# Streaming operands stored as two halves and read alternately, 16 columns from each

## The chip, the core and the metric

The kernel runs on one core of one Trainium2 chip. A core has a matrix engine (TensorE, called PE in the profile; its weight loads are listed apart, as PEld), three engines for elementwise work (VectorE = DVE, ScalarE = ACT, GpSimd = POOL), and queues that issue transfers (SP and POOL here). The on-chip memory that the engines read, SBUF, has 128 partitions; a tile [128, n] keeps n elements in each. Matrix results land in another memory, PSUM. The metric is the device time of one execution in microseconds: the median of three runs before the change is 1984.05 us (1983.36 to 1985.76).

A matrix instruction has two operands. One, 128 x 128 here, is loaded into the array and stays there (the *stationary* operand, the PEld rows). The other runs through the array column by column (the *streamed* or moving operand, 256 or 512 columns here). This case is about where the columns of the streamed operand lie in SBUF and in what order they are read.

## What is computed

One layer over 2048 tokens of width 1024, everything in float32:

```python
hl  = rms_norm(x) * A1 + sh1                      # A1, sh1 from the vector c and ada_w
b, cc, v = split(hl @ w_in, 3)                    # 1024 -> 3 x 1024
y   = (b * conv3(cc * v)) @ w_out
lat = x + g1 * y
h2  = rms_norm(lat) * A2 + sh2
aff = softmax(h2 @ router)                        # 16 experts
for e in range(16):                               # the 256 tokens with the highest aff[:, e]
    xs  = h2[idx[e]]
    hid = silu(xs @ w_gate[e]) * (xs @ w_up[e])
    out[idx[e]] += g2 * gate[e] * (hid @ w_down[e])
```

The kernel makes each large product in three parts. A float32 operand is split into a high part (written in the type float32r) and a low part (the rest), and high x high, low x high and high x low are summed in PSUM. So each operand exists twice, and each pair of tiles costs three matrix instructions.

## The kernel before

The work has four stages with large products, and the order of all instructions is written out by hand; each engine runs its own list in that order.

*Input projection* (`to_hl`, `in_mm`, `in_out`). Tokens are taken in four quarters of 512. `to_hl` transposes a normalised 128-channel slice of a quarter into PSUM (L383), and writes it as the tile `hl`: `t[:, 0]` is the high part, by ScalarE from PSUM (L386), `t[:, 1]` the low part, by VectorE or, for some tiles of the first quarter, by GpSimd (L389). `hl` is streamed, 512 columns at a time, against 128 x 128 pieces of `w_in` that are stationary (L436, L437, L439). This makes 2304 matrix instructions of 512 columns.

*Output projection and router* (`out_mm`, `router_mm`). Here the activations are stationary and the weight `w_out` is streamed, 512 columns at a time (L641, L642, L644; 768 instructions). Residual, second norm and router run behind it.

*Choice of tokens* (`search_few`, `search_all`, `slots`, `pick`). Thresholds are searched on VectorE and ScalarE; from 835 to 876 us of the span the matrix engine is busy for 10.7 of 41 us.

*Experts* (`gate_up`, `down`). For each of 16 experts the 256 chosen tokens are gathered and transposed into `xT` (`fetch`, L988 and L989). `gate_up` streams `xT`, 256 columns, against stationary pieces of `w_gate` and `w_up` (L1010, L1012, L1014; 6144 instructions). Its results go through L1020 to L1024 into `hT`, high and low. `down` holds `hT` stationary and streams `w_down`, 512 columns (L1032 to L1034; 1536 instructions).

Weights arrive as pieces of 128 x 1024 float32 in a list whose order is fixed: `load_piece` starts the transfer into `raw` (3 buffers), `split_high` copies it as the high part into `ws` (8 buffers, ScalarE, L198), `split_low` writes the low part (VectorE, now and then GpSimd, L208). A piece of `w_in`, `w_gate` or `w_up` is later stationary, a piece of `w_out` or `w_down` is streamed. In all of them the columns lie one behind the other, and every streamed operand is read as one run of 1024 or 2048 bytes per partition, for example

```python
t = hl_tile([P, 2, QT])
nc.tensor.matmul(ps[m], wh, t[:, 0], start=(k == 0), stop=False)
...
nc.tensor.matmul(o, w[:, 0, j, c0], xT[:, 0, k], start=(k == 0 and f % 2 == 0), stop=False,
...
nc.tensor.matmul(ps[s], h, w[:, 0, j], start=(k == 0), stop=False)
```

Of the kernel before, what the change touches and what calls it, by code (L numbers as in the profile page):

```python
# [16 lines left out]
P = 128  # L17
D = 1024
L = 2048
E = 16  # L20
CAP = 256
KD = D // P
NB = L // P
NQ = 4
QT = L // NQ
# [9 lines left out]

def dram(src, offset, ap):
    return bass.AP(tensor=src.tensor, offset=src.offset + offset, ap=ap)


@with_exitstack  # L40
def block_kernel(ctx: ExitStack, tc, x, c, ada_w, ada_b, norm_g, w_in, conv, w_out, router, wg, wu, wd, out):
    nc = tc.nc
    ctx.enter_context(tc.manual_schedule())
    consts = ctx.enter_context(tc.tile_pool(name="consts", bufs=1))
    wpool = ctx.enter_context(tc.tile_pool(name="weights", bufs=1))
# [3 lines left out]
    n_raw, n_split = 3, 8  # L49
# [39 lines left out]
    A1 = consts.tile([P, 8], F32, name="A1")  # L89
    sh1 = consts.tile([P, 8], F32, name="sh1")  # L90
# [77 lines left out]


    pieces, n_load, n_high, n_done = [], 0, 0, 0  # L170
    ws_of = {}
# [15 lines left out]
    def load_to(i):  # L187
        nonlocal n_load
        while n_load <= min(i, len(pieces) - 1, load_end[0] - 1):
            load_piece(n_load)  # L190
            n_load += 1

    def split_high(i):
        nonlocal n_high
        while n_high <= min(i, len(pieces) - 1):
            load_to(n_high)
            t = wpool.tile([P, 2] + pieces[n_high][3], F32R, name="ws", tag="ws", bufs=n_split)
            nc.scalar.activation(t[:, 0], raws[n_high], AF.Copy)  # L198
            ws_of[n_high] = t
            n_high += 1  # L200

    def split_low(i, eng=None, part=0, n=1):
        nonlocal n_done
        split_high(i)
        t, raw = ws_of[i], raws[i]
        w = pieces[i][3][-1] // n
        s = slice(part * w, (part + 1) * w)
        (eng or nc.vector).tensor_sub(t[:, 1, ..., s], raw[..., s], t[:, 0, ..., s].bitcast(F32))  # L208
        if part == n - 1:
            raws.pop(i)  # L210
            n_done += 1
            load_to(i + n_raw)

    def split_to(i, eng=None):
        while n_done <= min(i, len(pieces) - 1):
# [32 lines left out]
    w_o = [add_piece(w_out, k * P * D, [[D, P], [1, D]], [D]) for k in range(KD)]  # L248
    w_moe = {}

    def add_moe(m, e, h):
        for kk in range(KD // 2):
            for mm_ in (m if isinstance(m, tuple) else (m,)):
                w_moe[mm_, e, h, kk] = add_piece((wg, wu, wd)[mm_], (e * D + 2 * kk * P) * D + h * QT,
                                                 [[D, P], [P * D, 2], [1, QT]], [2, QT])

    for e in range(E + 1):
        for h in range(2):
# [89 lines left out]
    with tc.tile_pool(name="mix", bufs=1) as mix:  # L348
# [31 lines left out]
        def to_hl(q, k, between=lambda: None, eng=None):  # L380
            pt = tp.tile([P, QT], F32, name="pt", tag="tp")
            for b in range(4):
                nc.tensor.transpose(pt[:, b * P:(b + 1) * P], xq[q][b][:, k * P:(k + 1) * P], identf)  # L383
            full = m2("full")
            t = hl_tile([P, 2, QT])
            nc.scalar.activation(t[:, 0], pt, AF.Identity, scale=A1[:, k:k + 1], bias=sh1[:, k:k + 1])  # L386
            nc.scalar.activation(full, pt, AF.Identity, scale=A1[:, k:k + 1], bias=sh1[:, k:k + 1])
            between()
            (eng or nc.vector).tensor_sub(t[:, 1], full, t[:, 0].bitcast(F32))  # L389
            hl[q, k] = t  # L390

        ada_t, ada_a = {}, {}

# [36 lines left out]
            nc.vector.tensor_mul(A1[:, k:k + 1], A1[:, k:k + 1], g0_col[:, k:k + 1])  # L430

        def in_mm(ps, q, W, k):
            t = hl[q, k]
            for m in range(3):
                wh, wl = W(k, m)
                nc.tensor.matmul(ps[m], wh, t[:, 0], start=(k == 0), stop=False)  # L436
                nc.tensor.matmul(ps[m], wl, t[:, 0], start=False, stop=False)  # L437
            for m in range(3):
                nc.tensor.matmul(ps[m], W(k, m)[0], t[:, 1], start=False, stop=(k == KD - 1))  # L439

        def in_out(ps, q, ct):
            pb, pc, pv = ps
# [120 lines left out]
        before, ones_b, tri, slot_r, step, bias, need, zero1, cnts, aux, same, quick = constants(m2)  # L563
# [11 lines left out]
        for i, (ps_, ct, q) in enumerate(steps):  # L575
# [23 lines left out]
            ps = new_banks()  # L599
# [15 lines left out]
        def half(h):  # L615
            return slice(h * QT, (h + 1) * QT)
# [17 lines left out]
        def out_mm(tb, k, hs=(0, 1)):  # L634
            ps = ps_of.setdefault(tb, {})
            vh, vl = vs_of[tb]
            w = ws_of[w_o[k]]
            for h in hs:
                if k == 0:
                    ps[h] = mm.tile([P, QT], F32, name="pm", tag="mm")  # L640
                nc.tensor.matmul(ps[h], vh[:, k], w[:, 0, half(h)], start=(k == 0), stop=False)  # L641
                nc.tensor.matmul(ps[h], vh[:, k], w[:, 1, half(h)], start=False, stop=False)  # L642
            for h in hs:
                nc.tensor.matmul(ps[h], vl[:, k], w[:, 0, half(h)], start=False, stop=(k == KD - 1))  # L644

        def out_res(tb, h, soon=None):

# [343 lines left out]
    def gate_up(e, fh, between=lambda k: None):  # L991
        xT = xT_of[e]
        if fh == 0:
            hT_of[e] = {}
        ps = [[mm.tile([P, 2, CAP], F32, name="pm", tag="mm") for _ in range(2)] for _ in range(2)]
        for kk in range(KD // 2):
            for j in range(2):
                k = 2 * kk + j
                n = w_moe[0, e, fh, kk] + n_split - 2 + j
                if (e, fh) != (0, 1):  # L1000
                    split_high(n)
                between(k)
                while n_done <= min(n, len(pieces) - 1):
                    split_low(n_done, nc.gpsimd if n_done % 2 and (e, fh) < (1, 1) else None)
                for f in range(4):
                    c0 = slice(f * P, (f + 1) * P)
                    for m in range(2):
                        o = ps[m][f // 2][:, f % 2]
                        w = ws_of[w_moe[m, e, fh, kk]]
                        nc.tensor.matmul(o, w[:, 0, j, c0], xT[:, 0, k], start=(k == 0 and f % 2 == 0), stop=False,  # L1010
                                         skip_group_check=True)
                        nc.tensor.matmul(o, w[:, 0, j, c0], xT[:, 1, k], start=False, stop=False,  # L1012
                                         skip_group_check=True)
                        nc.tensor.matmul(o, w[:, 1, j, c0], xT[:, 0, k], start=False, stop=(k == KD - 1),  # L1014
                                         skip_group_check=True)
        hT = moe.tile([P, 2, 4, CAP], F32R, name="hT", tag="hT", bufs=4)
        hT_of[e][fh] = hT
        for f2 in range(2):
            sg = moe.tile([P, 2, CAP], F32, name="sg", tag="sg", bufs=2)
            nc.scalar.activation(sg, ps[0][f2], AF.Silu)  # L1020
            nc.vector.tensor_mul(sg, sg, ps[1][f2])
            t = slice(2 * f2, 2 * f2 + 2)
            nc.scalar.activation(hT[:, 0, t], sg, AF.Copy)
            nc.vector.tensor_sub(hT[:, 1, t], sg, hT[:, 0, t].bitcast(F32))  # L1024

    def down(e, dh, between=lambda kk: None):
        ps = [mm.tile([P, H], F32, name="pm", tag="mm") for _ in range(2)]

        def product(s, k):
            w, j, t = ws_of[w_moe[2, e, dh, k // 2]], k % 2, slice(s * P, (s + 1) * P)  # L1030
            h, l = (hT_of[e][k // 4][:, i, k % 4, t] for i in range(2))
            nc.tensor.matmul(ps[s], h, w[:, 0, j], start=(k == 0), stop=False)  # L1032
            nc.tensor.matmul(ps[s], h, w[:, 1, j], start=False, stop=False)  # L1033
            nc.tensor.matmul(ps[s], l, w[:, 0, j], start=False, stop=(k == KD - 1))  # L1034

        for kk in range(KD // 2):
            between(kk)
# [12 lines left out]
        c0 = slice(dh * H, (dh + 1) * H)  # L1050
# [75 lines left out]
```

## Time and profile before

| what | value |
|---|---|
| median of three runs | 1984.05 us |
| the profiled execution, whole | 1985.33 us |
| its span, first to last instruction | 1983.5 us |
| mean granted TensorE clock in the span | 0.982 |
| PE busy | 1901.4 us (96%) |
| PEld busy | 1669.5 us (84%) |
| DVE busy | 1130.6 us (57%) |
| ACT busy | 751.2 us (38%) |
| POOL busy | 306.9 us (15%) |
| moved by the transfers | 344.38 MB, 174 GB/s on average |

A row of a group of instructions reads: line of the kernel, engine, operation, tile written <- tiles read, shape, count | busy us, mean duration of one in ns | idle time of the engine just before them. Matrix instructions overlap in the array: the next starts while the last is still draining, so the duration of one is longer than the time from its start to the next one's start. It is that distance between starts that adds up to the length of a stage. The view of stretches gives for a window A:B its length, the busy time of each engine with the number of instructions that lie in it or are cut by its edges, the granted clock of the matrix engine (1.00 is full), the share of the transfer engines and GB/s. A row of the timeline gives the start in us from the span's start, the duration in us, and the instruction.

### The profile page before, as it was taken

The numbers are of one execution on the slowest core, as the hardware profiler recorded it, in microseconds if no ns is written. First come the engines' busy times: TensorE is split into PE (matmuls) and PEld (weight loads), VectorE is DVE, ScalarE is ACT, GpSimd is POOL, SyncE is SP. The second block draws the span as 40 slices with busy tenths as digits, with TensorE's granted clock in tenths as the row PEclk, the third lists the DMA queues.
The fourth block names the chain that finished last, engine by engine and source line by source line (L and its number), as shares of the span: only waits on it lengthen the run. The fifth ranks groups of instructions, "written<-read, shape, count | busy, mean of one in ns | idle before, by whom it ended". The sixth has DMA issues, their size and how long they took to land.

```text
span 1983.5 us, 29691 instructions
## 1 busy us (share of the span) xinstructions
PE 1901.4 (96%) x11930; PEld 1669.5 (84%) x11930; DVE 1130.6 (57%) x1656; ACT 751.2 (38%) x1050; POOL 306.9 (15%) x521
## 2 busy tenths in 40 slices
PE   4999999999999999659999999999999999999998
PEld 3787788887788888549999999999999999999996
DVE  7544424344334666776665656656665666566653
ACT  3411126211123333345444544444444444444542
POOL 3310011101011222333211011101110110111001
PEclk8999999999999999869999999999999999999999
DMA  9443241433216443235677676767677766777674
GB/s 283 127 133 127 81 144 53 139 127 123 67 64 213 166 149 132 85 127 165 199 222 211 214 233 200 220 217 235 202 214 233 227 201 214 229 209 218 212 212 116
DMA packets 216573, 344.38 MB, mean 174 GB/s; under 512 B 12092, under 2 KB 94068, under 8 KB 216436
## 3 DMA queue, kind: packets, MB, share of 16 engines
q1 hardware_dynamic: 200468, 284.82, 44.6%
q0 software_dynamic: 15968, 57.68, 11.2%
q8 instruction: 93, 1.52, 0.3%
q14 instruction: 44, 0.36, 0.1%
HBM read 300.51 MB, written 41.94 MB: 173 GB/s over the span
## 4 chain that ended last, share of the span: by engine, by line
PE 92%; DVE 3%; DMA 2%; SPq 1%; issue 1%; ACT 1%; POOL 0%; POOLq 0%; DVEq 0%; ACTq 0%
PE pm L1010 11%; PE pm L1012 11%; PE pm L1014 11%; PE pm L436 9%; PE pm L437 9%; PE pm L439 9%; PE pm L1032 6%; PE pm L1034 6%; PE pm L1033 6%; PE pm L641 3%; PE pm L644 3%; PE pm L642 3%; PE pt L986 1%; SPq L399 1%; DVE hl L312 1%
## 5 line engine op out<-in xcount | busy, mean ns | idle before, releaser
L208 DVE TENSOR_TENSOR ws<-raw,ws 128x1024 fp32r<-128x1024 f32 x415 | 499.0, 1223 | 314.4 <-ACT ws L198 312.5
L198 ACT ACTIVATE ws<-raw 128x1024 fp32r<-128x1024 f32 x437 | 451.0, 1054 | 444.2 <-PE pm L1014 208.0
L1010 PE MATMUL pm<-xT,ws 128*128 128x256 f32 x2048 | 569.6, 278 | 0.0
L1012 PE MATMUL pm<-xT,ws 128*128 128x256 f32 x2048 | 567.7, 277 | 0.1
L1014 PE MATMUL pm<-xT,ws 128*128 128x256 f32 x2048 | 567.4, 277 | 0.0
L1012 PEld LDWEIGHTS pm<-xT,ws 128*128 128x128 f32 x2048 | 386.4, 189 | 1.7 <-DVE xT L989 0.4
L1010 PEld LDWEIGHTS pm<-xT,ws 128*128 128x128 f32 x2048 | 386.2, 189 | 1.2
L1014 PEld LDWEIGHTS pm<-xT,ws 128*128 128x128 f32 x2048 | 386.0, 189 | 0.0
L436 PE MATMUL pm<-hl,ws 128*128 128x512 f32 x768 | 311.2, 405 | 1.0 <-ACT hl L386 1.0
L437 PE MATMUL pm<-hl,ws 128*128 128x512 f32 x768 | 307.0, 400 | 0.0
L439 PE MATMUL pm<-hl,ws 128*128 128x512 f32 x768 | 222.7, 398 | 0.0
L1032 PE MATMUL pm<-ws,hT 128*128 128x512 f32 x512 | 203.8, 398 | 0.0
L1034 PE MATMUL pm<-ws,hT 128*128 128x512 f32 x512 | 201.5, 394 | 0.0
L1033 PE MATMUL pm<-ws,hT 128*128 128x512 f32 x512 | 200.0, 391 | 0.0
L436 PEld LDWEIGHTS pm<-hl,ws 128*128 128x128 f32 x768 | 146.4, 191 | 36.6 <-ACT hl L386 1.4
L437 PEld LDWEIGHTS pm<-hl,ws 128*128 128x128 f32 x768 | 146.4, 191 | 35.1 <-issue 1.0
L439 PEld LDWEIGHTS pm<-hl,ws 128*128 128x128 f32 x768 | 145.8, 190 | 35.8
L1058 POOL DMA_INDIRECT out_dram<-ot,idx x32 | 78.5, 2454 | 591.4 <-DVE ot L1052 587.4
L449 DVE TENSOR_TENSOR u<-cs,pm 128x512 f32<-128x512 f32 x32 | 22.5, 703 | 246.0 <-ACT cs L446 246.0
L446 ACT ACTIVATE cs<-pm 128x512 f32<-128x512 f32 x32 | 19.1, 597 | 346.8 <-issue 272.0
L1034 PEld LDWEIGHTS pm<-ws,hT 128*128 128x128 f32 x512 | 96.2, 188 | 20.7
L1033 PEld LDWEIGHTS pm<-ws,hT 128*128 128x128 f32 x512 | 96.3, 188 | 18.9
(267 smaller groups left out, 2026.8 us busy)
## 6 DMA issues: line engine op xcount, KB each, us to landing
raw<-in_moe_w_gate_dram SPq DMA_DIRECT2D x128, 512.0 KB, 4.4
raw<-in_moe_w_up_dram SPq DMA_DIRECT2D x128, 512.0 KB, 4.3
raw<-in_moe_w_down_dram SPq DMA_DIRECT2D x128, 512.0 KB, 4.6
raw<-in_sc_w_in_dram SPq DMA_DIRECT2D x45, 512.0 KB, 4.6
xt<-in_x_dram SPq DMA_DIRECT2D x32, 512.0 KB, 6.2
aw<-in_ada_w_dram SPq DMA_DIRECT2D x32, 512.0 KB, 6.5
hl<-in_ada_w_dram SPq DMA_DIRECT2D x32, 256.0 KB, 5.4
hl<-vscr SPq DMA_DIRECT2D x16, 512.0 KB, 5.0
```

The source lines that it names most:

```text
L198: nc.scalar.activation(t[:, 0], raws[n_high], AF.Copy)
L208: (eng or nc.vector).tensor_sub(t[:, 1, ..., s], raw[..., s], t[:, 0, ..., s].bitcast(F32))
L436: nc.tensor.matmul(ps[m], wh, t[:, 0], start=(k == 0), stop=False)
L437: nc.tensor.matmul(ps[m], wl, t[:, 0], start=False, stop=False)
L439: nc.tensor.matmul(ps[m], W(k, m)[0], t[:, 1], start=False, stop=(k == KD - 1))
L1010: nc.tensor.matmul(o, w[:, 0, j, c0], xT[:, 0, k], start=(k == 0 and f % 2 == 0), stop=False, skip_group_check=True)
L1012: nc.tensor.matmul(o, w[:, 0, j, c0], xT[:, 1, k], start=False, stop=False, skip_group_check=True)
L1014: nc.tensor.matmul(o, w[:, 1, j, c0], xT[:, 0, k], start=False, stop=(k == KD - 1), skip_group_check=True)
L1032: nc.tensor.matmul(ps[s], h, w[:, 0, j], start=(k == 0), stop=False)
L1033: nc.tensor.matmul(ps[s], h, w[:, 1, j], start=False, stop=False)
L1034: nc.tensor.matmul(ps[s], l, w[:, 0, j], start=False, stop=(k == KD - 1))
L1058: st = nc.gpsimd.indirect_dma_start(out=out_rows, out_offset=bass.IndirectOffsetOnAxis(ap=idx_of[e][:, s:s + 1], axis=0), in_=ots[s], in_o ...
```

## The change

Each operand that is streamed is stored in another order. A row of n columns is cut into blocks of 16; blocks 0, 2, 4, ... go to the first half of the tile's row, blocks 1, 3, 5, ... to the second half. `streamed` is the view of such a row in the original order: 16 columns from the first half, 16 from the second, the next 16 from the first, and so on. The distance between the two halves is 1024 bytes for `hl` (512 columns), 512 bytes for `xT` (256 columns) and 2048 bytes for a weight piece (1024 columns).

```diff
+def streamed(t):
+    return t.rearrange("p (h j i) -> p j h i", h=2, i=16)
+
+def in_blocks(t):
+    return t.rearrange("p (j h i) -> p j h i", h=2, i=16)
...
-    def add_piece(src, offset, ap, shape):
+    def add_piece(src, offset, ap, shape, streams=False):
+        if streams:
+            moving.add(len(pieces))
...
-            t = wpool.tile([P, 2] + pieces[n_high][3], F32R, name="ws", tag="ws", bufs=n_split)
-            nc.scalar.activation(t[:, 0], raws[n_high], AF.Copy)
+            if n_high in moving:
+                t = wpool.tile([P, 2, D], F32R, name="ws", tag="ws", bufs=n_split)
...
+                raws[n_high] = raw = in_blocks(raw)
+                nc.scalar.activation(streamed(t[:, 0]), raw, AF.Copy)
+            else:
+                t = wpool.tile([P, 2] + pieces[n_high][3], F32R, name="ws", tag="ws", bufs=n_split)
+                nc.scalar.activation(t[:, 0], raws[n_high], AF.Copy)
...
+        high, low = (streamed(t[:, m]) if i in moving else t[:, m] for m in range(2))
+        (eng or nc.vector).tensor_sub(low, raw, high.bitcast(F32))
...
+    def stream_of(i, j):
+        return tuple(streamed(ws_of[i][:, m])[:, j * QT // 32:(j + 1) * QT // 32] for m in range(2))
...
+        mix.tile([P, 56], F32, name="mixpad")
...
+            high, low = streamed(t[:, 0]), streamed(t[:, 1])
+            nc.scalar.activation(high, in_blocks(pt), AF.Identity, scale=A1[:, k:k + 1], bias=sh1[:, k:k + 1])
...
+            (eng or nc.vector).tensor_sub(low, in_blocks(full), high.bitcast(F32))
+            hl[q, k] = high, low
...
-                nc.tensor.matmul(ps[m], wh, t[:, 0], start=(k == 0), stop=False)
+                nc.tensor.matmul(ps[m], wh, high, start=(k == 0), stop=False)
...
+            w = [stream_of(w_o[k], h) for h in range(2)]
...
+    moe.tile([P, 48], F32, name="moepad")
...
+                xh, xl = (streamed(xT[:, i, k]) for i in range(2))
...
-                        nc.tensor.matmul(o, w[:, 0, j, c0], xT[:, 0, k], start=(k == 0 and f % 2 == 0), stop=False,
+                        nc.tensor.matmul(o, w[:, 0, j, c0], xh, start=(k == 0 and f % 2 == 0), stop=False,
...
-        hT = moe.tile([P, 2, 4, CAP], F32R, name="hT", tag="hT", bufs=4)
+        hT = moe.tile([P, 2, 2, 2, 2, P], F32R, name="hT", tag="hT", bufs=4)
...
+            sg = in_blocks(sg.rearrange("p f t -> p (f t)"))
+            high, low = (streamed(hT[:, i, f2].rearrange("p s f t -> p (s f t)")) for i in range(2))
+            nc.scalar.activation(high, sg, AF.Copy)
+            nc.vector.tensor_sub(low, sg, high.bitcast(F32))
...
+            w = stream_of(w_moe[2, e, dh, k // 2], k % 2)
+            h, l = (hT_of[e][k // 4][:, i, k % 4 // 2, s, k % 2] for i in range(2))
```

Who writes what: for `hl` and for the pieces of `w_out` and `w_down`, the elementwise instructions that split high from low now write (and, for the low part, also read the high part) in blocks of 16; the streaming then meets the columns in their original order. `xT` is written as before, 128 tokens behind 128 tokens; the streaming mixes the two halves, so the 256 result columns of `gate_up` stand in another order, and the two instructions that write `hT` (L1023, L1024) write in blocks of 16 and so restore it. The stationary slices of `hT` remain 128 columns in one run. No instruction is added or removed. Two unused tiles of 56 and 48 floats, `mixpad` and `moepad`, shift the tiles allocated behind them, `hl` and `xT` among them, by 224 and 192 bytes.

More of the change, by code (lines that the diff above doesn't have):

```diff
@@ L247, in block_kernel @@
                 w_chan[ps_, ct, m] = add_piece(w_in, m * D + ct * P, [[3 * D, P], [3 * D * P, KD], [1, P]], [KD, P])
-    w_o = [add_piece(w_out, k * P * D, [[D, P], [1, D]], [D]) for k in range(KD)]
+    w_o = [add_piece(w_out, k * P * D, [[D, P], [1, D]], [D], True) for k in range(KD)]
     w_moe = {}
@@ L640, in out_mm @@
                     ps[h] = mm.tile([P, QT], F32, name="pm", tag="mm")
-                nc.tensor.matmul(ps[h], vh[:, k], w[:, 0, half(h)], start=(k == 0), stop=False)
-                nc.tensor.matmul(ps[h], vh[:, k], w[:, 1, half(h)], start=False, stop=False)
+                nc.tensor.matmul(ps[h], vh[:, k], w[h][0], start=(k == 0), stop=False)
+                nc.tensor.matmul(ps[h], vh[:, k], w[h][1], start=False, stop=False)
             for h in hs:
-                nc.tensor.matmul(ps[h], vl[:, k], w[:, 0, half(h)], start=False, stop=(k == KD - 1))
+                nc.tensor.matmul(ps[h], vl[:, k], w[h][0], start=False, stop=(k == KD - 1))
         def out_res(tb, h, soon=None):
@@ L1029, in product @@
         def product(s, k):
[L1030 to L1034, printed above, removed]
+            w = stream_of(w_moe[2, e, dh, k // 2], k % 2)
+            h, l = (hT_of[e][k // 4][:, i, k % 4 // 2, s, k % 2] for i in range(2))
+            nc.tensor.matmul(ps[s], h, w[0], start=(k == 0), stop=False)
+            nc.tensor.matmul(ps[s], h, w[1], start=False, stop=False)
+            nc.tensor.matmul(ps[s], l, w[0], start=False, stop=(k == KD - 1))
         for kk in range(KD // 2):
```

37 lines of the change are left out of this document (14 added, 23 removed).

## The prediction

> **What bounds the kernel now.** I read the page first: busy times, the slices, the chain that ended last. Then the list of what the matrix engine waited for, then stretches of each stage, and last the timeline inside them.
>
> ```profile
> span 1983.5 us, 29691 instructions
> PE 1901.4 (96%) x11930; PEld 1669.5 (84%) x11930; DVE 1130.6 (57%) x1656; ACT 751.2 (38%) x1050; POOL 306.9 (15%) x521
> ...
> PE   4999999999999999659999999999999999999998
> ...
> PE 92%; DVE 3%; DMA 2%; SPq 1%; issue 1%; ACT 1%; POOL 0%; POOLq 0%; DVEq 0%; ACTq 0%
> ```
>
> PE is busy in every slice but the first and those near 840 us, and 92% of the chain is PE. Its longest waits in total are these:
>
> ```profile
> PE pc L323 <- DVE each L319: 23.4, 7, 5.8
> PE pcol L423 <- DVE acc L416: 18.7, 5, 8.0
> PE pc L865 <- ACT hit L859: 5.7, 5, 2.8
> ```
>
> They belong to the start and to the choice of tokens, where nothing that the change touches is at work except `to_hl` at the start. In the large stages PE doesn't wait; only the time that each matrix instruction takes counts. "Busy" doesn't tell that time, because instructions overlap, so I count starts in stretches that hold one kind only: input projection (twice), half-clock gate-up, gate-up, a slower piece of gate-up, and down.
>
> ```profile
> core 0: us, PE busy (x), PEclk, DMA share, GB/s
> 85.00:169.00 84.00, 84.00 (x360) 1.00 0.35 116
> 348.00:448.00 100.00, 100.00 (x428) 1.00 0.42 137
> 876.00:880.00 4.00, 3.87 (x18) 0.50 0.14 52
> 1040.00:1060.00 20.00, 20.00 (x179) 1.00 0.69 233
> 978.00:991.00 13.00, 13.00 (x113) 1.00 0.78 276
> 1943.00:1973.00 30.00, 30.00 (x133) 1.00 0.42 93
> ```
>
> ```profile
> 877.29 0.41 PE L1010 MATMUL pm<-xT,ws 128*128 128x256 f32 x1
> ...
> 879.64 0.41 PE L1014 MATMUL pm<-xT,ws 128*128 128x256 f32 x1
> ```
>
> ```profile
> 711.18 0.39 PE L642 MATMUL pm<-ws,hl 128*128 128x512 f32 x1
> 711.42 0.39 PE L641 MATMUL pm<-ws,hl 128*128 128x512 f32 x1
> 711.65 0.40 PE L642 MATMUL pm<-ws,hl 128*128 128x512 f32 x1
> 711.88 0.63 PE L644 MATMUL pm<-ws,hl 128*128 128x512 f32 x2
> 712.35 0.22 PE L708 MATMUL plt<-hl,rts 128*32 128x128 f32 x1
> ```
>
> The count of a stretch takes in what its edges cut: an instruction of 0.39 us with starts 0.23 us apart adds 1.7, one of 0.28 us with starts 0.11 us apart adds 2.4. So the distance between starts is 100/426.3 = 234.6 ns in the input projection, (712.35 - 711.18)/5 = 234 ns in the output projection, 30/131.3 = 228.5 ns in down (all 512 columns), and 20/176.6 = 113.3 ns in gate-up (256 columns). At half clock the 11 steps from 877.29 to 879.64 give 213.6 ns for 256 columns, 0.834 ns a column; at full clock the same count of array cycles would be 0.417 ns a column: 106.8 ns for 256 and 213.6 ns for 512. That is the floor. So today a 512-column instruction loses 15 to 21 ns and a 256-column one 6.5 ns on something that isn't there at half clock. Within a stage it is steady: the input projection gives 84/358.3 = 234.4 ns early and 234.6 ns later. And gate-up has two rhythms for the very same tiles: 113.3 ns, and 13/110.6 = 117.5 ns from 978 to 991 us. I take this to be the reading of the streamed operand, which at full clock is at the edge of what its way out of SBUF gives. The trace doesn't say more, and no matrix instruction in it reads its streamed operand in blocks.
>
> **The change part by part.**
>
> *The streamed reads* are the whole matter: counts from the page.
>
> ```profile
> L1010 PE MATMUL pm<-xT,ws 128*128 128x256 f32 x2048 | 569.6, 278 | 0.0
> ...
> L436 PE MATMUL pm<-hl,ws 128*128 128x512 f32 x768 | 311.2, 405 | 1.0 <-ACT hl L386 1.0
> ...
> L1032 PE MATMUL pm<-ws,hT 128*128 128x512 f32 x512 | 203.8, 398 | 0.0
> ```
>
> Each line has two more like it, so 6144, 2304 and 1536; the output projection has 3 x 256 = 768. Going to and fro between two halves can do two things. It can take away the loss, if this comes from successive blocks of one run meeting in the same part of SBUF, or from the streamed run overtaking the load of the next weights there. Or it can cost at each of its jumps: 32 in 512 columns, 16 in 256. Nothing in the trace prices a jump. Lower bound: the floor of 213.6 and 106.8 ns. Upper bound, from the row that is nearest: one array cycle of 0.417 ns a jump on top of today's distance, 13.3 and 6.7 ns.
>
> I take the side of the gain. The loss exists, is regular, is not the array's own (half clock) and depends on the rhythm (113.3 against 117.5 ns), which is how a meeting of two periodic reads behaves; and reading in another order changes just that. How far? For 512 columns I take the middle between the floor, 213.6, and the best that a full-clock stream does today, twice gate-up's 113.3 = 226.6: 220 ns. For 256 columns I take a third of the way from 113.3 to 106.8, 111 ns, since in gate-up the weight loads run without a gap too, and may hold the rhythm by themselves:
>
> ```profile
> core 0: us, PE busy (x) PEld busy (x) DVE busy (x) ACT busy (x) POOL busy (x), PEclk, DMA share, GB/s
> 1039.00:1059.00 20.00, 20.00 (x179) 20.00 (x178) 10.19 (x10) 7.61 (x8) 0.00 (x0) 1.00 0.69 233
> 1106.00:1930.00 824.00, 824.00 (x6221) 772.97 (x6221) 507.58 (x585) 377.92 (x436) 83.74 (x58) 1.00 0.71 217
> ```
>
> The terms: input projection 2304 x (234.6 - 220) = 33.6 us; output projection 768 x (234 - 220) = 10.8; down 1536 x (228.5 - 220) = 13.1; gate-up 6144 x (113.3 - 111) = 14.1. Sum 71.6 us.
>
> The Trainium skill, "TensorE: Matmul & The Clock Gate", section "Wait — 56ns, not 53.3ns?", gives for matmuls back to back N / 1.2 GHz cold and N / 2.4 GHz + 2.5 ns warm, 215.7 ns for 512 columns; the half-clock row agrees (213.6 ns for 256), the full-clock rows lie 13 to 19 ns above. By that rule, as an estimate, all four stages together would give back some 102 us rather than 72, and the time would be about 1882 us.
>
> *The elementwise writes in blocks.* ScalarE and VectorE write `hl`, 136 weight pieces and `hT` in runs of 16. The nearest rows are the two that write `xT`: four runs of 128, beside the two that write one run of 512.
>
> ```profile
> L988 ACT ACTIVATE xT<-pt x64: 573/594/601, 872.4 to 1884.5; 128x512 fp32r<-128x512 f32 x64
> L691 ACT ACTIVATE hl<-pt x32: 577/598/601, 626.2 to 825.6; 128x512 fp32r<-128x512 f32 x32
> L989 DVE TENSOR_TENSOR xT<-pt,xT x64: 675/683/692, 874.0 to 1885.6; 128x512 fp32r<-128x512 f32 x64
> L389 DVE TENSOR_TENSOR hl<-full,hl x28: 680/692/2840, 21.3 to 350.4; 128x512 fp32r<-128x512 f32 x28
> L389 POOL TENSOR_TENSOR hl<-full,hl x4: 1283/1291/1299, 51.0 to 66.5; 128x512 fp32r<-128x512 f32 x4
> L208 DVE TENSOR_TENSOR ws<-raw,ws x415: 1209/1224/1509, 107.6 to 1955.8; 128x1024 fp32r<-128x1024 f32 x139
> ```
>
> 594 against 598 and 683 against 692 ns: runs cost nothing there. If a run of 16 doubled each, VectorE between 1106 and 1930 us would get some 100 pieces x 1.22 + 50 x 0.69 = 157 us on top of 508 of 824, still with room. Only in the first 62 us would it show: eight tiles x 0.78 us (ScalarE) and four x 1.29 us (GpSimd), up to 11 us. I take 0, with 0 to +11 for the range; a gain isn't excluded, but the durations that exist leave nothing to gain.
>
> *Pads, and the order of columns in `gate_up`.* No instruction. The pads move where `hl` and `xT` start in a partition; whether a start matters no row shows, so its price is within the bounds of the streamed reads. PSUM is written in one run as before; `hT`'s stationary slices stay whole, so the weight loads of down stay as they are.
>
> *What becomes late next.* If PE is 4% faster, VectorE rises from 62% (507.58/824) to 64%, and the transfers from a share of 0.71 to 0.74 in the expert stage; neither is full, and a piece is split several products ahead. In the output projection VectorE is the next:
>
> ```profile
> 620.00:820.00 200.00, 200.00 (x1094) 160.87 (x1092) 130.21 (x237) 63.28 (x151) 52.11 (x160) 1.00 0.41 145
> ```
>
> 65% there. I take nothing off for it.
>
> Sum: the profiled execution of 1985.33 us (span 1983.5 and 1.8 around it) becomes 1985.3 - 71.6 = 1913.7; the median of the runs is 1.3 us lower than that execution, so 1912 us.
>
> **The rivals.**
>
> *The jumps cost (slower).* Place: the streaming of all 10752 large matrix instructions. If each of the jumps between the halves costs an array cycle and the loss stays, 4608 x 13.3 + 6144 x 6.7 = 102 us: 2086 us. For it: the streams already run at the edge, and a broken run is the harder one to fetch ahead. Against it: the blocks of 16 are long, and the `xT` writers take broken runs for nothing. Were the loss given back as I forecast, it decides from 71.6/102 = 0.7 cycle a jump.
>
> *Gate-up falls into its slow rhythm, the rest stays (slower).* The 117.5 ns rhythm of 978 to 991 us becomes the rule: 6144 x 4.2 = 26 us, 2010 us. For it: both rhythms occur today with equal tiles, so little decides between them. Against it: the fast one holds in the later stretch quoted, 1040 to 1060 us.
>
> *Nothing happens.* The loss is one of rate and a block of 16 is as good as a run: 1984 us. The Trainium skill, "SBUF — State Buffer", section "Door 1: The DMA port swizzle", says that SBUF is read in lines of 16 bytes and that a penalty falls on each step to a new line; since 16 columns are four whole lines, as many lines are read as before, and by that rule this rival would be it. No run here shows lines.
>
> *How the numbers follow.* Gain in the streams 0.62, slow rhythm 0.11, jumps cost 0.22, nothing 0.05. The gain's own range: at best all streams reach the floor: 2304 x 21 + 768 x 20.4 + 1536 x 14.9 + 6144 x 6.5 = 127 us, 1857; at least the 512-column ones reach 226.6 and gate-up nothing: 18.4 + 5.7 + 2.9 = 27 us, 1957. The range over all cases runs from 1865 to 2060: it leaves out the last of the floor case and the dearer half of the jumps, whose price is not bounded above by a row. A measurement of this kernel tells about 0.2% (4 us) from no change; so faster 0.62, same 0.05, slower 0.33.
>
> **What would show it.** In the changed profile: starts of the input projection's instructions 220 ns apart (under 226 or I am wrong on the size, over 234 on the sign), gate-up 111, down 220; the ScalarE and VectorE rows for `ws`, `hl`, `hT` within 3% of today's; the first 62 us unchanged, and no new waits of PE on `ws` or `raw`. Wrong would be the forecast if the distances rise by a multiple of the jumps (13 and 7 ns), or if they fall and new PE waits on `ws` or `raw` take the gain.

## The result and the profile after

The change makes the kernel slower: 2053.3 us (2052.37 to 2053.74) against 1983.94 us (four runs each), a ratio of 1.0347, 95% interval 1.0329 to 1.0365. The profiled execution takes 2052.37 us, its span 2050.6 us, 67.1 us more than before. From the page after; the columns are those of before:

```profile
span 2050.6 us, 29691 instructions
PE 1972.1 (96%) x11930; PEld 1719.3 (84%) x11930; DVE 1130.1 (55%) x1656; ACT 748.4 (36%) x1050; POOL 307.3 (15%) x521
...
PE 93%; DVE 4%; issue 1%; ACT 1%; DMA 1%; POOL 0%; SPq 0%; POOLq 0%; DVEq 0%; ACTq 0%
```

The number of instructions is the same, VectorE and ScalarE are busy as long as before, and all the added time is PE's. The distances between starts tell it. Stretches of the profile after, input projection, gate-up, down (length, PE busy and its count, granted clock, DMA share, GB/s):

```profile
87.00:171.00 84.00, 84.00 (x351) 1.00 0.35 116
1094.00:1115.00 21.00, 21.00 (x178) 1.00 0.82 218
2009.00:2039.00 30.00, 30.00 (x127) 1.00 0.37 88
```

and the output projection in the timeline:

```profile
732.93 0.40 PE L665 MATMUL pm<-ws,hl 128*128 128x512 f32 x1
...
735.33 0.65 PE L668 MATMUL pm<-ws,hl 128*128 128x512 f32 x2
```

With the same allowance for instructions that the edges cut: 84/349.3 = 240.5 ns, 21/175.6 = 119.6 ns, 30/125.3 = 239.4 ns, and (735.33 - 732.93)/10 = 240 ns. Before it was 234.6, 113.3, 228.5 and 234. A count is a whole number, and one more or less in it moves these distances by 0.7 to 2 ns. So every stream now runs at 240 ns for 512 columns and 120 for 256, the same in all stages, about 9/8 of the floor of 213.6 and 106.8. The terms: 2304 x 5.9 + 6144 x 6.3 + 1536 x 10.9 + 768 x 6 = 74 us. The span shows 67; some of gate-up had already run at half clock or in the slow rhythm before, and lost less. About half of the sum is gate-up.

The elementwise writes in blocks cost nothing. After, ScalarE's copy of a piece in a run (L219) and in blocks (L216):

```profile
L219 ACT ACTIVATE ws<-raw 128x1024 fp32r<-128x1024 f32 x301 | 308.2, 1051 | 185.4 <-DMA raw<-in_moe_w_up_dram 88.4
L216 ACT ACTIVATE ws<-raw 128x1024 fp32r<-128x1024 f32 x136 | 140.0, 1055 | 288.1 <-PE pm L1040 218.6
```

1055 against 1051 ns for a piece. The high part of `hT` takes 632 ns on average as before (L1023, after L1050), the low part 741 ns as before (L1024, after L1051). VectorE's busy time over the whole span is 1130.1 us, as it was 1130.6.

### The profile page after: what moved, and what is told of

It is laid out like the page before. It is cut to its first block, busy times and chain, and to the rows that moved or that the text cites. A ratio compares the mean times of both kernels' runs of the same rounds, so it can differ in the third digit from the quotient of the medians.

```text
span 2050.6 us, 29691 instructions
## 1 busy us (share of the span) xinstructions
PE 1972.1 (96%) x11930; PEld 1719.3 (84%) x11930; DVE 1130.1 (55%) x1656; ACT 748.4 (36%) x1050; POOL 307.3 (15%) x521
## 4 chain that ended last, share of the span: by engine, by line
PE 93%; DVE 4%; issue 1%; ACT 1%; DMA 1%; POOL 0%; SPq 0%; POOLq 0%; DVEq 0%; ACTq 0%
PE pm L1036 12%; PE pm L1038 12%; PE pm L1040 12%; PE pm L460 9%; PE pm L461 9%; PE pm L463 9%; PE pm L1059 6%; PE pm L1061 6%; PE pm L1060 6%; PE pm L665 3%; PE pm L668 3%; PE pm L666 3%; PE pt L1011 1%; DVE hl L334 1%; PE pt L714 1%
## 5 line engine op out<-in xcount | busy, mean ns | idle before, releaser
L1036 PE MATMUL pm<-xT,ws 128*128 128x256 f32 x2048 | 580.8, 284 | 0.0
L1038 PE MATMUL pm<-xT,ws 128*128 128x256 f32 x2048 | 579.1, 283 | 0.1
L1040 PE MATMUL pm<-xT,ws 128*128 128x256 f32 x2048 | 579.0, 283 | 0.0
L219 ACT ACTIVATE ws<-raw 128x1024 fp32r<-128x1024 f32 x301 | 308.2, 1051 | 185.4 <-DMA raw<-in_moe_w_up_dram 88.4
L460 PE MATMUL pm<-hl,ws 128*128 128x512 f32 x768 | 316.3, 412 | 0.9 <-ACT hl L410 0.9
L461 PE MATMUL pm<-hl,ws 128*128 128x512 f32 x768 | 312.2, 406 | 0.0
L216 ACT ACTIVATE ws<-raw 128x1024 fp32r<-128x1024 f32 x136 | 140.0, 1055 | 288.1 <-PE pm L1040 218.6
L463 PE MATMUL pm<-hl,ws 128*128 128x512 f32 x768 | 227.4, 405 | 0.0
L1059 PE MATMUL pm<-ws,hT 128*128 128x512 f32 x512 | 209.7, 409 | 0.0
L1061 PE MATMUL pm<-ws,hT 128*128 128x512 f32 x512 | 206.3, 403 | 0.0
L1060 PE MATMUL pm<-ws,hT 128*128 128x512 f32 x512 | 206.3, 403 | 0.0
L460 PEld LDWEIGHTS pm<-hl,ws 128*128 128x128 f32 x768 | 148.4, 193 | 38.7 <-ACT hl L410 1.3
L463 PEld LDWEIGHTS pm<-hl,ws 128*128 128x128 f32 x768 | 148.1, 193 | 38.0
L461 PEld LDWEIGHTS pm<-hl,ws 128*128 128x128 f32 x768 | 148.5, 193 | 37.4 <-issue 1.0
L1061 PEld LDWEIGHTS pm<-ws,hT 128*128 128x128 f32 x512 | 97.7, 191 | 25.1
```

The lines of the kernel that those rows point to most:

```text
L216: nc.scalar.activation(streamed(t[:, 0]), raw, AF.Copy)
L460: nc.tensor.matmul(ps[m], wh, high, start=(k == 0), stop=False)
L461: nc.tensor.matmul(ps[m], wl, high, start=False, stop=False)
L463: nc.tensor.matmul(ps[m], W(k, m)[0], low, start=False, stop=(k == KD - 1))
L1036: nc.tensor.matmul(o, w[:, 0, j, c0], xh, start=(k == 0 and f % 2 == 0), stop=False, skip_group_check=True)
L1038: nc.tensor.matmul(o, w[:, 0, j, c0], xl, start=False, stop=False, skip_group_check=True)
```

## The experiments

The theory of the prediction was that the old loss is a meeting in SBUF, of the streamed operand with itself or with something else, which another order avoids. The sign speaks against it. Three readings of the 240 ns are left at this point: the old loss is gone and each jump costs (A), the old loss stays and the jumps add to it (B), or any broken pattern runs at 9/8 (C). A fourth (D) came with the run of the pads alone: what counts is where the streamed row lies against the weights that are being loaded.

**The parts, and the length of a run.** First the pads alone, then the interleaved reads alone, then the whole change with longer runs (32 or 64 also in `in_blocks`, and the counts in `stream_of` to match).

```diff
 pads    +        mix.tile([P, 56], F32, name="mixpad")
         +    moe.tile([P, 48], F32, name="moepad")          # kernel before, nothing else
 nopads  the changed kernel without these two lines
 blk32   -    return t.rearrange("p (h j i) -> p j h i", h=2, i=16)
         +    return t.rearrange("p (h j i) -> p j h i", h=2, i=32)
 blk64   +    return t.rearrange("p (h j i) -> p j h i", h=2, i=64)
```

> The kernel before with the two unused tiles alone (56 and 48 floats), each streamed operand still one run. If a start inside a 64-byte block is what costs the input and output projection more (234 ns) than down (228.5 ns): both come down to about 229 ns, 2304 x 5.5 + 768 x 5 = 16 us, 1968 us. If the start doesn't matter: 1984 us and the same distances as before.

> The changed kernel without its two unused tiles: only the interleaved reads in runs of 16 remain. If the two parts of the change simply add, the pads' 31 us go: about 2022 us. If the interleaved read has a price of its own wherever the tiles start: 240 and 120 ns, 2053 us. If it is the place of the streamed operand against the place of the weights (the pads changed it) that sets everything: distances of their own in each stage, gate-up back near 113 ns.

> The changed kernel with runs of 32 columns from each half in place of 16. Theory A (each jump between runs costs two array cycles, 0.83 ns, and the loss of the one-run stream is gone once it is broken): starts 213.3 + 16 x 0.83 = 226.7 ns apart for 512 columns and 113.3 ns for 256, about 1956 us. Theory B (the old loss stays, and the jumps add the difference measured: 5.5 ns per 32 jumps, 6.5 ns per 16 in gate-up): half the added time goes, about 237 and 117 ns, 2020 us. Theory C (any streamed operand whose pattern has several dimensions goes at 9/8 of the array time, whatever the run length): 240 and 120 ns, 2053 us.

> The changed kernel with runs of 64 columns. Theory A: 213.3 + 8 x 0.83 = 220 ns for 512 columns, 110 ns for 256, if the weight loads allow it: about 1904 us, faster than before. Theory B: a quarter of the added time stays: about 236 and 115 ns, 2001 us. Theory C: 240 and 120 ns, 2053 us.

Measured: pads alone 2016.23 us (ratio 1.0158, 1.0141 to 1.0175); interleaved reads alone 2054.88 us (1.0351, 1.0333 to 1.037); runs of 32 2038.28 us (1.0269, 1.0252 to 1.0286); runs of 64 2016.62 us (1.0165, 1.0148 to 1.0182). Only the interleaved reads alone came out as one of the cases expected; the others were missed. The pads, to which I had given no price of their own, cost 32 us by themselves. In their profile the stretches of input projection, gate-up and down read (the two rows behind them are the input projection and gate-up with runs of 32):

```profile
350.00:430.00 80.00, 80.00 (x346) 1.00 0.44 142
1001.00:1022.00 21.00, 21.00 (x179) 1.00 0.85 218
1980.00:2004.00 24.00, 24.00 (x105) 1.00 0.43 90
...
352.00:452.00 100.00, 100.00 (x424) 1.00 0.42 137
...
1048.00:1068.00 20.00, 20.00 (x169) 1.00 0.66 223
```

80/344.3 = 232.4 ns, 21/176.6 = 118.9 ns and 24/103.3 = 232.3 ns: the input projection gains 2 ns, gate-up loses 5.6 and down 4, by nothing but 224 and 192 bytes of shift. The interleaved reads alone already give 2055 us, so the two parts don't add: with runs of 16 it is 240 and 120 ns with the pads and without. Runs of 64 from two halves behave as one run does at the same starts (2016.6 against 2016.2 us). So the price isn't one of the dimensions of the pattern (theory C falls), and the old loss didn't go away for longer runs (theory A falls). Runs of 32 lie between: 100/422.3 = 236.8 ns for 512 columns, which theory B has, but 20/166.6 = 120 for 256, which it hasn't. So B doesn't hold as it stands either.

**Four patterns in one kernel.** The kernel before with `mixpad`; only `hl` is changed, with another order in each quarter `q` of the tokens.

```diff
+        PAT = (('p (h j i) -> p j h i', 'p (j h i) -> p j h i', dict(h=2, i=8)), ('p (j h i) -> p h j i', 'p (h j i) -> p h j i', dict(h=2, i=16)), ('p (h j i) -> p j h i', 'p (j h i) -> p j h i', dict(h=4, i=16)), ('p (h j i) -> p j h i', 'p (j h i) -> p j h i', dict(h=2, i=128)))
+
+        def runs_of(q, t):
+            return t.rearrange(*PAT[q][0:1], **PAT[q][2])
...
-            nc.scalar.activation(t[:, 0], pt, AF.Identity, scale=A1[:, k:k + 1], bias=sh1[:, k:k + 1])
+            high, low = runs_of(q, t[:, 0]), runs_of(q, t[:, 1])
+            nc.scalar.activation(high, plain(q, pt), AF.Identity, scale=A1[:, k:k + 1], bias=sh1[:, k:k + 1])
```

> The kernel before with mixpad, and only the input projection's streamed operand changed, in another way for each quarter of the tokens: quarter 0 in runs of 8 from two halves, quarter 1 in runs of 16 taken upward with every second run skipped (jumps of 64 bytes, never back), quarter 2 in runs of 16 from four quarters of the row in turn, quarter 3 in runs of 128 from two halves. Theory A (a price for each jump): 213.3 + 64 x 0.83 = 266.7, 240, 240 and 216.7 ns. A price by address (reading to and fro between two far places): quarter 1 near 234, quarter 2 unlike the changed kernel's 240. Theory C: 240 in all four.

Each row below is the first matrix instruction of a step; a step has 72 with one pattern, so the difference to the next step's first, over 72, is the distance.

```profile
120.88 0.41 PE L446 MATMUL pm<-hl,ws 128*128 128x512 f32 x1
138.40 0.41 PE L446 MATMUL pm<-hl,ws 128*128 128x512 f32 x1
155.69 0.41 PE L446 MATMUL pm<-hl,ws 128*128 128x512 f32 x1
...
373.81 0.40 PE L446 MATMUL pm<-hl,ws 128*128 128x512 f32 x1
390.80 0.39 PE L446 MATMUL pm<-hl,ws 128*128 128x512 f32 x1
407.52 0.39 PE L446 MATMUL pm<-hl,ws 128*128 128x512 f32 x1
423.85 0.39 PE L446 MATMUL pm<-hl,ws 128*128 128x512 f32 x1
```

Runs of 8, to and fro: 243.3 ns, not 266.7. Runs of 16 taken upward with every second one left out, and those left out on a second pass, so that there is one step back in the middle of the row: 240.1. Runs of 128: 232.2. Runs of 16 from four quarters in turn: 236.0 in the step from 373.81 and 226.8 in the one from 407.52, on the same tiles with the same pattern (its last four steps show 233.3). With twice the jumps the price hardly rises, with as many jumps it is 240 or as little as 226.8, and with a single step back in place of fifteen it stays. A price for each jump, the rival of the prediction, is refuted as well as theory A.

**The place of the weights.** The pads had shown that starts count. The next kernel (`scan`) leaves the streams alone and shifts the stationary operand of each step of the input projection by 32 bytes more.

```diff
-            return lambda k, m: tuple(ws_of[w_chan[ps_, ct, m]][:, j, k] for j in range(2))
+                row = ws_of[w_chan[ps_, ct, m]][:, j].rearrange("p k n -> p (k n)")
+                c0 = k * P + shift - (P if shift and k == KD - 1 else 0)
+                return row[:, c0:c0 + P]
...
-                in_mm(ps, q, W_chan(ps_, ct), k)
+                in_mm(ps, q, W_chan(ps_, ct, 8 * (i % 16)), k)
```

> The kernel before, but in the input projection each of the 30 steps (one step is 72 matrix instructions with one weight triple and one quarter) takes its stationary 128 columns from a start shifted by 32 bytes more than the step before, over 512 bytes and then again; it multiplies by the wrong columns of w_in, so its time is read and not its result. Theory D (what counts is the place of the weights that are being loaded against the place of the streamed row, modulo 256 bytes): the distance between starts changes from step to step with a period of 8 steps, from about 226.7 ns (64 bytes behind, as in gate-up before; shifts of 224 and 480) to 229 (64 ahead, as in down before; 96 and 352) and 232.5 (half of 256; 32 and 288). Theory E (only the start of the streamed row itself counts): 234 ns in all steps.

First instructions of five successive steps, with shifts 0, 32, 64, 96 and (the next) 128 bytes; then the first and the third from the last of the step with shift 416:

```profile
363.53 0.39 PE L436 MATMUL pm<-hl,ws 128*128 128x512 f32 x1
380.39 0.39 PE L436 MATMUL pm<-hl,ws 128*128 128x512 f32 x1
397.12 0.39 PE L436 MATMUL pm<-hl,ws 128*128 128x512 f32 x1
413.92 0.40 PE L436 MATMUL pm<-hl,ws 128*128 128x512 f32 x1
430.41 0.40 PE L436 MATMUL pm<-hl,ws 128*128 128x512 f32 x1
...
584.35 0.39 PE L436 MATMUL pm<-hl,ws 128*128 128x512 f32 x1
...
599.99 0.84 PE L439 MATMUL pm<-hl,ws 128*128 128x512 f32 x3
```

234.2, 232.4, 233.3 and 229.0 ns; then 15.64/69 = 226.7 ns. The pattern repeats every 8 steps, that is every 256 bytes. In the addresses that the program gives its tiles, `hl` starts 32 bytes above a multiple of 256 before the change and a piece of weights 128 above one, so a shift s puts the stream at -96 - s against the weights, modulo 256:

| stream against weights, bytes mod 256 | 0 | 32 | 64 | 96 | 128 | 160 | 192 | 224 |
|---|---|---|---|---|---|---|---|---|
| shift | 160, 416 | 128 | 96 | 64 | 32 | 0 | 224 | 192 |
| distance, ns | 226.7 | 233.3 | 229.0 | 233.4 | 232.4 | 234.2 | 233.4 | 233.2 |

The same table explains the stages of the kernel before: the input projection stands at 160 (234.2), the output projection at 96 (234) and down at 64 (228.5). I had expected the best at 192, by gate-up's 113.3; it is at 0, and 192 is ordinary for 512 columns.

The same scan on the changed kernel:

> The changed kernel with the same scan of the weights' place, result not that of the layer for the same reason. Streamed in runs of 16 from two halves, the row moves on through the low address bits at half the pace, as fast as the weights that are being loaded. Theory D: at some shifts the two never meet and the distance falls near the floor (214 to 220 ns), at others they meet all the time (240). A price of the jumps alone, or of the pattern: 240 ns at every shift.

```profile
390.20 0.40 PE L460 MATMUL pm<-hl,ws 128*128 128x512 f32 x1
407.48 0.40 PE L460 MATMUL pm<-hl,ws 128*128 128x512 f32 x1
```

17.28/72 = 240.0 ns, and so at all 16 shifts. The place of the weights makes no difference to the stream in runs of 16.

**Trains of one kind.** To measure patterns apart from the kernel, trains of 42 matrix instructions stand behind its end, each on a line of its own:

```diff
     down(E - 1, 1)
+    xf = xT_of[E - 1][:, 0].rearrange("p k c -> p (k c)")
+    wf = hT_of[E - 1][0][:, 0].rearrange("p f c -> p (f c)")
+    o = mm.tile([P, QT], F32, name="pm", tag="mm")
+    for n in range(42): nc.tensor.matmul(o, wf[:, 0:128], xf[:, 0:512], start=(n == 0), stop=(n == 41))
...
```

> The kernel before, and behind its end 31 trains of 42 matrix instructions whose results nobody reads, so its time is longer by them and only the distances in each train are read. One-run streams of 512 columns, place of the stream against that of the weights 0, 64, 128 bytes: theory D 226.7, 229, 232.5 ns; with a load of only 32 columns in place of 128, theory D expects the loss over the floor of 213.6 (216 with a fixed part) to shrink to a quarter or so; if the stream loses by itself, it stays at 227 to 233. Runs of 16 from two halves: if the price of the interleaved read is the stream's own, 240 ns with a load of 32 columns too; if it is a meeting with the load, about 220. Halves 64, 128, 192 bytes farther apart than 1024: if the price comes from both halves having the same low address bits, these fall to 227 to 234; if each alternation costs, 240 at every distance. 256 columns at 8 places: gate-up's 113.3 ns at 0 or 192, and 117 to 120 at 128; a place below 113 would be new.

A row is a train: its start, its whole duration. The next train's start less its own, over 42, is the distance; where the next one isn't shown, it is the duration less the 0.39 us of the last instruction, over 41. The last row below is from the view of stretches and takes in nearly all trains; behind PE and PEld it has VectorE, ScalarE and GpSimd, then the granted clock and the transfers' share.

```profile
1970.78 9.71 PE L1107 MATMUL pm<-xT,hT 128*128 128x512 f32 x42
1980.33 9.79 PE L1109 MATMUL pm<-xT,hT 128*128 128x512 f32 x42
1989.96 9.92 PE L1111 MATMUL pm<-xT,hT 128*128 128x512 f32 x42
1999.72 9.89 PE L1113 MATMUL pm<-xT,hT 128*32 128x512 f32 x42
2009.44 9.85 PE L1115 MATMUL pm<-xT,hT 128*32 128x512 f32 x42
...
2038.39 9.34 PE L1121 MATMUL pm<-xT,hT 128*128 128x512 f32 x42
2047.58 5.19 PE L1123 MATMUL pm<-xT,hT 128*128 128x256 f32 x42
...
2137.78 10.24 PE L1149 MATMUL pm<-xT,hT 128*32 128x512 f32 x42
2147.86 10.24 PE L1151 MATMUL pm<-xT,hT 128*128 128x512 f32 x42
...
1982.00:2222.00 240.00, 240.00 (x1191) 188.58 (x1190) 0.00 (x0) 0.00 (x0) 0.00 (x0) 1.00 0.00 1
```

The last row settles a rival that the kernel itself leaves open: that other engines or transfers take SBUF's time from the stream. While the trains run, the elementwise engines do nothing and the transfers' share is 0.00, and the distances are those of the kernel.

One run at places 0, 64, 128 (L1107, L1109, L1111): 227, 229, 232 ns, as the scan gave. With weights of 32 columns in place of 128 (L1113, place 0, and L1115, place 128): 231 ns both. With weights that are one column read 128 times (L1119, place 0) it is 229 ns. So the loss doesn't shrink with the load of the weights; no train is without a load, but a quarter of it leaves all of the loss, and the place of the load only chooses among values between 227 and 234. That is where theory D, as a meeting of stream and load, falls; what stays of it is the table. A stream that reads one and the same column 512 times (L1121) takes 219 ns, so most of the loss goes with walking through addresses. Runs of 16 from two halves (L1149, weights of 32 columns): 240 ns, and equally with weights of 128, with halves 1024, 1088, 1152, 1216 or 2048 bytes apart, with a start moved by 32 bytes, and when every second run of a longer row is taken and none is read backward (L1163). So neither equal low address bits nor the load nor a step back makes the price. Four parts in turn take 232 to 236 ns by their distance and start, eight in turn 239. 256 columns gave 117 to 120 ns at all eight places; gate-up's 113.3 did not appear.

**Starts by the table.** The streams stay whole; two other pads put stream and weights at place 0 in three stages.

```diff
+        mix.tile([P, 24], F32, name="mixpad")               # starts and mix24
...
+        if (e, fh) == (0, 0):                               # starts only, ahead of hT
+            moe.tile([P, 16], F32, name="moepad")
```

> The kernel before with one-run streams and two other unused tiles, 24 floats ahead of hl and 16 ahead of hT, so that in the input projection, the output projection and down the streamed row and the weights being loaded start at the same place modulo 256 bytes; gate-up stays. Theory D, by the scan: 226.7 ns in all three (from 234.3, 233.4 and 229.0): 2304 x 7.6 + 768 x 6.7 + 1536 x 2.3 = 26 us, about 1958 us. If the scan's differences came from the shifted weights alone and not from the relation to the stream: 1984 us.

Measured 1984.88 us, ratio 1.0007 (0.9997 to 1.0017): nothing. Stretches of input projection, gate-up (twice), down:

```profile
350.00:430.00 80.00, 80.00 (x355) 1.00 0.42 137
...
879.00:886.00 7.00, 7.00 (x64) 1.00 0.65 215
...
1017.00:1038.00 21.00, 21.00 (x181) 1.00 0.70 225
...
1945.00:1970.00 25.00, 25.00 (x112) 1.00 0.45 106
```

80/353.3 = 226.4 and 25/110.3 = 226.7 ns, as forecast. But gate-up, whose own tiles (`xT` and the pieces) stand where they stood, has gone from 113.3 to 21/178.6 = 117.6 ns, into its slow rhythm, and 6144 x 4.3 = 26 us are given back. The second row is a piece of gate-up ahead of the first down: there the fast rhythm still occurs, 7/61.6 = 113.6 ns. That points to the stage ahead. Two runs test this: the same without the pad at `hT`, so that down keeps its old rhythm; and trains of 256 columns at place 192 behind trains of 512 at places 0, 64 and 128.

> The kernel before with one unused tile of 24 floats ahead of hl and nothing else: stream and weights start at the same place modulo 256 bytes in the input and output projection, while hT and gate-up stay as they were. If gate-up lost its fast rhythm in the run with both tiles because down's rhythm, from which it starts, had changed: down stays at 229, gate-up at 113.7 ns, and 2304 x 7.2 + 768 x 4.7 = 20 us are kept, 1964 us. If gate-up loses it by whatever is changed earlier: 1984 us again.

Measured 1963.66 us against 1982.79 us, ratio 0.9902 (0.9885 to 0.9919): faster than both kernels; 1% is small, but the interval is clear of 1. Its input projection and gate-up:

```profile
350.00:430.00 80.00, 80.00 (x355) 1.00 0.44 142
...
1018.00:1039.00 21.00, 21.00 (x188) 1.00 0.71 236
```

226.4 ns and 21/185.6 = 113.1 ns: the gain of the two projections is kept. The two runs differ in 64 bytes by which `hT`, and behind it the elementwise tiles `sg` and `ot`, move. So gate-up's rhythm here hangs on down's place or on that of `sg` and `ot`; no run separates the two in the kernel. The trains below show that what runs ahead can do it alone.

> The kernel before with other trains behind its end, time not read. Six trains of 256 columns at one and the same place (192 bytes, as in gate-up), each right behind a train of 512 columns at place 64 (down before), 0 or 128. If the rhythm is settled by how the train is entered: about 113.3 ns behind one of them and 117 to 120 behind others, the same again in the repeat; if the place alone settles it: one value for all. Broken runs, upward with gaps: if each end of a run costs a fixed time, the loss over 213.6 ns doubles with half the run length; if what is fetched is a block of 64 or 128 bytes and each block costs one more clock, runs of 16 with gaps stay at 240 and runs of 64 at 227, and columns taken 8 or 16 bytes apart cost several times as much.

Trains of 60 times 256 columns, all at one place, behind trains at place 0 (L1109), 64 (L1113) and 128 (L1117); then runs of 16 with a stride of 24 columns (L1139), of 48 (L1141) and of 64 (L1143), runs of 32 with a stride of 36 (L1145), runs of 64 with a stride of 128 (L1153), of 4 with a stride of 8 (L1159), of 2 with a stride of 4 (L1161), single columns 2 apart (L1163), and each block of 16 read twice (L1169):

```profile
1980.02 7.23 PE L1109 MATMUL pm<-xT,hT 128*128 128x256 f32 x60
...
1993.97 7.23 PE L1113 MATMUL pm<-xT,hT 128*128 128x256 f32 x60
...
2008.02 6.96 PE L1117 MATMUL pm<-xT,hT 128*128 128x256 f32 x60
...
2096.61 9.97 PE L1139 MATMUL pm<-xT,hT 128*128 128x512 f32 x42
2106.41 10.15 PE L1141 MATMUL pm<-xT,hT 128*128 128x512 f32 x42
2116.40 10.24 PE L1143 MATMUL pm<-xT,hT 128*128 128x512 f32 x42
2126.48 9.97 PE L1145 MATMUL pm<-xT,hT 128*128 128x512 f32 x42
...
2165.68 9.73 PE L1153 MATMUL pm<-xT,hT 128*128 128x512 f32 x42
...
2194.84 9.87 PE L1159 MATMUL pm<-xT,hT 128*128 128x512 f32 x42
2204.55 19.22 PE L1161 MATMUL pm<-xT,hT 128*128 128x512 f32 x42
2223.59 19.22 PE L1163 MATMUL pm<-xT,hT 128*128 128x512 f32 x42
...
2271.97 10.24 PE L1169 MATMUL pm<-xT,hT 128*128 128x512 f32 x42
```

An instruction of 256 columns ends 0.28 us after its start, so the first two trains have (7.23 - 0.28)/59 = 117.8 ns and the third (6.96 - 0.28)/59 = 113.2; the repeat of the six gave the same three durations. Equal instructions on equal addresses keep one of two rhythms through all 60 of a train, by what ran ahead of them. The rule isn't simply "down at 64 gives the fast one", though: in the kernel gate-up is fast behind down at place 64, here only behind 128. What at the entry decides stays open.

Runs of 16 give 240 ns with strides of 20 and 64 columns and also when each block is read twice in place, but 233 with a stride of 24 and 238 with one of 48; runs of 64 with a stride of 128 give 228, as one run does, runs of 4 with a stride of 8 231. So the loss is no multiple of the ends of runs, and a pattern of several dimensions need not cost. Of the runs tried, only those of 2 columns (8 bytes) or 1 change the scale: 453 ns.

## Why the prediction was wrong

The sign was wrong, and with it the time: 1912 us forecast, 2053.3 measured, inside the range of all cases (1865 to 2060) but on the side given 0.33.

*What bounds the kernel* held: PE's distance between starts is the whole of it; no wait, no other engine moved. *The counts and the distances before* held. *The elementwise writes*, priced at 0 with +11 at most: 1055 against 1051 ns for a piece, right. *What becomes late next*: nothing had the chance, since PE became slower.

The step that failed is "I take the side of the gain": that the loss comes from a meeting in SBUF, which another order would avoid. Its term, 71.6 us to be gained on the streamed reads, came out as some 74 us lost by the same sum. The trains show that the stream has its loss with all other engines idle and with a quarter of the weight load (231 ns), and that runs of 16 from two halves have a loss of their own over the floor, 26.4 ns in 512 columns and 13.2 in 256, that no distance between the halves, no start and no load that was tried changes. Interleaved reads without the pads cost as much (2054.88 us), so this is what made the kernel slower. The half-clock argument showed only that there is a loss at full clock, not that it is avoidable. The two rhythms of gate-up, which I read as a sign that order helps, had to do with what runs ahead; and the rows of before already showed 234.6 and 228.5 ns for the same 512 columns, which is the difference of starts in the table.

*The rival of the jumps* got the sign right and nearly the time (2086 forecast), for the wrong reason: 32 jumps at 0.42 ns on top of the old loss would have been 248 ns, it was 240; runs of 8, with 64 jumps, cost 243.3; four quarters in turn, with as many jumps, cost 226.8 to 236. That gate-up's 120 is what this rival gives (113.3 + 6.7) is luck: runs of 32, with half the jumps, gave 120 too. *The rival of gate-up's slow rhythm* fell short: gate-up went past its 117.5 to 120, and the rest did not stay. Its rhythm did come in the run with better starts (117.6). *Nothing happens* is refuted by the 3.5%. The Trainium skill, "SBUF — State Buffer", section "Door 1: The DMA port swizzle", has a threshold of two hits a line of 16 bytes. The trains do show a step, but at another height: four float32 columns of every second 16 bytes cost no more than one run (231 ns), two of each four cost double (453 ns). Blocks of 16 columns are well above that step, and still were not free.

*Pads*: "its price is within the bounds of the streamed reads" was true and useless. Alone they cost 32 us: they put gate-up and down at place 128, and gate-up went to 118.9 ns, down to 232.3. For down that is the table's value. For gate-up the table says nothing, since it is for 512 columns. A train of 256 columns at place 128 has about the same (118.6), but it is not excluded that gate-up's rhythm came from down's new place.

*The warm rule* of the Trainium skill, "TensorE: Matmul & The Clock Gate", section "Wait — 56ns, not 53.3ns?", 215.7 ns for 512 columns, was reached by no stream here that walks through addresses. The best of them had 226.4 to 226.7 ns.

Open: what in the read path makes the loss; why runs of 16 sit at 240 ns, about 9/8 of the floor, while those at a stride of 24 or from four quarters in turn don't; and what at a train's entry picks its rhythm.

## What to carry to other kernels

When a matrix engine is busy all the time, measure the distance between starts and compare it with the same stream at half clock; but a loss that is seen there need not be one that can be taken away. Before data are re-ordered for it, try the start addresses: here 96 bytes of unused space ahead of one tile gave 1.0%, and re-ordering lost 3.5%. Check the stage behind the one you speed up: in the trains equal instructions on equal addresses ran at 113 or 118 ns by what had run ahead of them.

## What the runs showed that I had not expected

A streamed float32 row of 512 columns takes 226.7 to 234.2 ns by its place against the weights modulo 256 bytes, and 231 with weights of a quarter the size, all other engines idle; one column read 512 times takes 219. For 256 columns two rhythms, 113.2 and 117.8 ns, hold for 60 instructions on end. Runs of 16 columns from two halves take 240 ns at every distance, start and load that was tried, and so do runs of 16 at strides of 20, 32 and 64 columns; at strides of 24 and 48 it is 233 and 238. Runs of two columns cost 453 ns.
